# Third pair by quarters, more weight sums by adding transfers, and three more turns of zeros in a tuned encoder block

## The chip, the cores and the metric

The kernel runs on one core of one Trainium2 chip, in one launch. The time is device microseconds of that core, the median of three runs. The engines named below are PE (the matrix engine; PEld is its weight load), DVE (vector), ACT (scalar), POOL (GpSimd) and SP, whose queue issues the loads.

## The reference

The block works on 512 positions of 1024 features in float32:

```python
h = h + 0.5 * swiglu(rmsnorm(h, ffn1_norm), ffn1_w_in, ffn1_w_out)   # "first layer", D_FF = 2816
z = rmsnorm(h, mix_norm) @ w_in
h = h + concat([conv_module(z...), gated_linear_attention(z...)]) @ w_out
h = h + 0.5 * swiglu(rmsnorm(h, ffn2_norm), ffn2_w_in, ffn2_w_out)   # "second layer"
h = h + sigmoid(rmsnorm(h, ple_norm) @ w_gate) * (p @ w_proj)
out = rmsnorm(h, final_norm)

def swiglu(x, w_in, w_out):
    gate, up = split(x @ w_in, 2)
    return (silu(gate) * up) @ w_out
```

The change touches the two `swiglu` layers and the start of the kernel.

## The kernel before

**Numbers in two parts.** A float32 operand is held as a high part (rounded to the type that PE multiplies fast) and a low part, the rest. A product is three matmuls: high by high, high by low, low by high. The high part of a weight tile is a cast on ACT (`high`, tile `wh`), the low part a subtraction on DVE (`low`, tile `wl`). In place of DVE's subtraction stands in some places `added`: ACT writes the negated raw tile into `wl`, rounded by that tile's type, and POOL issues a transfer that adds the raw tile there, which leaves the rest:

```python
def added(w):
    h3, l3, r3 = w
    act.mul(l3, r3, -1.0)
    pool.dma_start(out=l3.bitcast(F32), in_=r3, accum_op=ALU.add)
    return w
```

An added low part costs ACT one more pass and DVE nothing, and the raw tile stays taken until the transfer has landed.

**Pairs.** The 2816 hidden features are 22 blocks of 128. Two blocks of gate and the two of up make a pair; there are eleven, numbered 0 to 10. A pair's product (1024 x 512 of weights by 1024 x 512 of x) is done in one of two ways:

- *Plain* (`plain_unit`, units `h0` to `h7`): eight units of 12 matmuls with 512 columns. A unit's weights are one of four raw tiles `a11`, `a12` (gate, features 0 to 511 and 512 to 1023), `a21`, `a22` (up).
- *By quarters* (Winograd's form of Strassen's product, units `m1` to `m7`, in the order m1, m2, m6, m7, m5, m4, m3, with the m1 and m2 of the next pair in between): seven products of 24 matmuls with 256 columns. It needs sums of weights (`s1` = a21 + a22 and `s2` = s1 - a11 in tiles `sm`; `s3` = a11 - a21 and `s4` = a12 - s2 in place in the raw tile) and sums of x (`t1` to `t4`, made by `Right` once for a layer: `pieces` on ACT, `sums1` and `sums2` on DVE, all in tiles `xg`, then `split` into two parts). `m1`, `m6`, `m5` and `m3` add up in one bank of PSUM, and ACT copies its state out after m1 (`sq`), m6 (`u2`, the tile `u` in the profile) and m5 (`sq`). The next product that adds into the bank waits for the copy.

Pair 0 is special in both layers and done before the others. Behind each pair its product goes through silu, the gate and a split (`act_parts`, tiles `actH`, `actL`); groups of two pairs then go through pieces of the second projection (`second`), 24 matmuls of 512 columns each, called blocks below, which are interleaved with the units. Each block adds into `h` by DVE.

**Order.** PE, ACT and DVE run in the order in which the program calls them, and so does SP. `drive` walks a list of units; every unit names jobs ("before") with a distance: a job of distance 4 is called four units ahead. Within a unit's turn the jobs go first, larger distance first, then what the last unit left over (its silu or product), then the unit's matmuls and the copy behind them, then its hook.

```python
before = [(AHEAD + (kind == 'm5'), lambda: p.part(part))] if part else []
...
before += [(9, lambda: p.fetch("a21", "a22")), (6, p.s12)]
```

AHEAD is 4. `part` is `high` and `low`, `add_part` is `high` and `added`. Raw weights have six buffers, `wh` and `wl` six each, PSUM seven banks and one more.

In the first layer (`ffn` with plain `(1, 2)`) pairs 1 and 2 are plain and quarters start at pair 3; in the second (plain `()`) quarters start at pair 1. At the start `warm_up` lets PE turn an identity tile while x loads (ten turns, then four), and the units `take` do pair 0 as x comes in.

All engine calls go through the class `Ordered`, so nearly every instruction of the profile stands under line L46, and one tells them apart by their tiles: `wh<-wr` is a cast of a raw weight tile, `wl<-wr,wh` a low part, `wl<-sm,wh` that of s1 or s2, `sm<-` the sums s1 and s2, `wr<-` s3 and s4, `hgH,wh` matmuls with x itself, `t1H` to `t3H` those with its sums, `actH,wh` blocks of the second projection, `ax<-ident` the turns of zeros.

Of the kernel before, what the change touches and what calls it, by code (L numbers as in the profile page):

```python
# [62 lines left out]
def block_kernel(ctx: ExitStack, tc: tile.TileContext, a: dict, out: bass.AP):  # L63
# [16 lines left out]
    def nm(s):  # L80
        uid[0] += 1
        return f"{s}_{uid[0]}"
# [10 lines left out]
    def tmp(s, w=SEQ, dt=F32, bufs=2):  # L93
        return tp.tile([P, w], dt, tag=s, bufs=bufs, name=nm(s))

    def bank():
        return pp.tile([P, SEQ], F32, tag="mm", bufs=7, name=nm("ps"))

    def aux():
        return pp.tile([P, SEQ], F32, tag="aux", bufs=1, name=nm("ax"))  # L100
# [15 lines left out]
    def columns(names, n, tile_name, queue):  # L116

        row = cp.tile([n, P], F32, name=tile_name + "r")
        col = cp.tile([P, n], F32, name=tile_name)
        r0 = 0  # L120
        for name, m in names:
            queue.dma_start(out=row[r0:r0 + m, :], in_=a[name][0].rearrange("(r p) -> r p", p=P))
            for c in range(m):
                vcols[name, c] = col[:, r0 + c:r0 + c + 1]
            r0 += m

        def turn():
            ps = aux()
            pe.transpose(ps[:, 0:n], row, ident[:n, :n])
            dve.tensor_copy(col, ps[:, 0:n])  # L130

        return turn
# [7 lines left out]
    def warm_up(n):  # L140
        idle = aux()
        for _ in range(n):
            pe.transpose(idle[:, 0:P], ident, ident)

    warm_up(10)
    turn_vec = columns(vecs[:1], 8, "vcol1", nc.scalar)

    def split(src, s, alloc=bt):
# [34 lines left out]
    def high(r3):  # L183

        nk, nc_ = r3.shape[1], r3.shape[2]
        hi = wp.tile([P, 1024], F32R, tag="wh", bufs=6, name=nm("wh"))
        lo = wp.tile([P, 1024], F32R, tag="wl", bufs=6, name=nm("wl"))
        h3 = hi[:, :nk * nc_].rearrange("p (k c) -> p k c", k=nk)
        l3 = lo[:, :nk * nc_].rearrange("p (k c) -> p k c", k=nk)
        act.copy(h3, r3)  # L190
        return h3, l3, r3

    def low(w, engine=dve):
        h3, l3, r3 = w
        engine.tensor_tensor(out=l3, in0=r3, in1=h3.bitcast(F32), op=ALU.subtract)
        return h3, l3
# [62 lines left out]
    def spread(col, copy=True):  # L259

        ps = aux()
        for j in range(TB):
            pe.transpose(ps[:, j * P:(j + 1) * P], col[:, j:j + 1].to_broadcast([P, P]), ident)
        if not copy:
            return ps
        bc = tmp("bc", bufs=1)
        act.copy(bc, ps)
        return bc
# [17 lines left out]
    class Norm:  # L286
        def __init__(self, engine=dve):
            self.engine = engine
            self.acc = bt(s="sqacc")
            self.n = 0  # L290
# [17 lines left out]
    def mul(ps, w, x, first, last, ks=range(4)):  # L308

        (wh, wl), k0 = w, ks[0]  # L310
        for k in ks:
            xh, xl = x[k]
            for i in range(2):
                cs = slice(i * P, (i + 1) * P)
                o = ps[:, i * HALF:(i + 1) * HALF]
                end = last and k == ks[-1] and i == 1
                pe.matmul(o, wh[:, k - k0, cs], xh, start=(first and k == ks[0] and i == 0), stop=False, skip_group_check=True)
                pe.matmul(o, wh[:, k - k0, cs], xl, start=False, stop=False, skip_group_check=True)
                pe.matmul(o, wl[:, k - k0, cs], xh, start=False, stop=end, skip_group_check=True)
# [68 lines left out]
    class Left:  # L388


        def __init__(self, w, f):
            self.w, self.f, self.done = w, f, {}

        def fetch(self, *names):
            for name in names:
# [10 lines left out]
        def part(self, name, engine=None):  # L406

            if name not in self.done:
                self.done[name] = low(high(getattr(self, name)), engine or dve)
            return self.done[name]  # L410

        def add_part(self, *names):

            for name in names:
                self.done[name] = added(high(getattr(self, name)))[:2]
# [21 lines left out]
    ffn1_in = a["ffn1_w_in"][0]  # L437
    hT = [big.tile([P, SEQ], F32, tag="H", bufs=DC, name=nm("h")) for _ in range(DC)]
    hg, xps, xt, squares = [], [], {}, []
# [12 lines left out]
    def turn_x(c):  # L452
        ps = bank()
        for t in range(TB):
            pe.transpose(ps[:, t * P:(t + 1) * P], xt[c][t], ident)
        xps.append(ps)
# [57 lines left out]
    w1 = Left(ffn1_in, 2)  # L514
# [5 lines left out]
        nc.sync.dma_start(out=made[2][i * RANK:(i + 1) * RANK, :], in_=a["gate_w_up"][0])  # L520
    turn_vec()
    turn_x(0)
    warm_up(4)
    ps0 = [bank() for _ in range(4)]
    split_w(0, 1, dve.tensor_copy)
    split_x(0)
    mid = []
# [22 lines left out]
    xb = Right(hg, "ffn1_norm")  # L550
    steps = xb.steps()
# [30 lines left out]
    AHEAD = 4  # L582
# [18 lines left out]
        for f in left:  # L601
            f()

    def ffn(w_in, w_out, x, gname, given, first, rsb, hooks, plain):


        norm = Norm()
# [3 lines left out]
        start = 1 + len(plain)  # L611
        held = []
        end = npair - 1
        pairs = {i: given.get(i) or Left(w_in, 2 * i) for i in range(npair)}
# [9 lines left out]
        def silu(g):  # L624
            s = tmp("s")
            act.activation(s, g, AF.Silu)
            return s
# [37 lines left out]
        def m2(p):  # L665
            p.y = bank()
            mul(p.y, p.part("a12"), x.op["b21"], True, True)

            def gate0():
                p.s0 = silu(plus(p.y, p.a, 0, "g1"))  # L670

            if p is pairs[start] and not plain:
                held.append(gate0)
                return []
            return [gate0]
# [51 lines left out]
        def unit(kind, i):  # L727
            p = pairs[i]

            def go(run):  # L730
                left = run(p)
                hooks.get((kind, i), lambda *_: None)()
                return left

            if kind[0] == "h":
                j = int(kind[1])
                part, run = (f"a{1 + j // 4}{1 + j % 2}", plain_unit(j)) if j % 4 < 2 else (None, plain_unit(j))
                if part:
                    return [(AHEAD, lambda: p.part(part)), (9, lambda: p.fetch(part))], lambda: go(run)
            else:  # L740
                part, run = USES[kind]
            before = [(AHEAD + (kind == 'm5'), lambda: p.part(part))] if part else []
            if kind in ("m1", "m2"):
                before.append((7, lambda: p.fetch(part)))
            elif kind == "m6":
                before += [(9, lambda: p.fetch("a21", "a22")), (6, p.s12)]
            elif kind in ("m7", "m3"):
                before.append((6, p.s3_ if kind == "m7" else p.s4_))

            return before, lambda: go(run)  # L750
# [80 lines left out]
        for i in range(start, npair):  # L831
# [3 lines left out]
            if i == end:  # L835
                half, rest = second(cut_of[i])
# [30 lines left out]
    w_in = a["w_in"][0]  # L867
    w_ahead = []

    def sums_hooks(x, names, at):  # L870

        h = {}
        for name, key in zip(names, at):
            h[key] = lambda *_, name=name: x.split(name)
        return h

    hooks = sums_hooks(xb, ("t2", "t3", "t1", "t4"), (("h5", 1), ("h7", 1), ("h3", 2), ("m1", 3)))
    hooks.update({("h%d" % (i + 1), 1): f for i, f in enumerate(steps[2:])})
    hooks.update({("m5", 3): lambda *_: made[0](), ("m5", 4): lambda *_: constants(),
                  ("m4", 10): lambda *_: w_ahead.append(ahead(w_in, D_CONV, 2 * P)),  # L880
                  ("last", 4): lambda *_: w_ahead.append(ahead(w_in, 0, 2 * P))})
    hg, norm = ffn(ffn1_in, a["ffn1_w_out"][0], xb, "mix_norm", {0: Left(ffn1_in, 0), 1: w1},
                   (ps0[:2], ps0[2:]), lambda: spread(mid[0]), hooks, (1, 2))
    pool.on = False
    cw, gwu, mean, mask, nbias = made

# [61 lines left out]
    mid = []  # L948
# [10 lines left out]
    rs, rsb = mid  # L959
# [16 lines left out]
    for k0 in range(0, DC, 4):  # L976
        for i in range(2):
            for j in range(4):
                pe.matmul(ps[2 * RANK * j:2 * RANK * (j + 1)], gw[:, k0 + j, :], hg[k0 + j][i].bitcast(F32),
                          start=(k0 == i == 0), stop=(k0 + i == 5), skip_group_check=True)  # L980
# [337 lines left out]
    ffn2_in = a["ffn2_w_in"][0]  # L1318
    wf = {i: Left(ffn2_in, 2 * i) for i in range(3)}
    w0, w1 = wf[0], wf[1]  # L1320
# [40 lines left out]
    norm = Norm()  # L1361
# [26 lines left out]
    for k in range(4):  # L1388
        for n in range(3):
            w, ps = half[n]  # L1390
# [28 lines left out]
    hg = nhg  # L1419
# [11 lines left out]
    mid = []  # L1431
    xb = Right(hg, "ffn2_norm")
    steps = xb.steps()
    steps[0]()
    w1.fetch("a21", "a22")
    w2 = wf[2]
    w2.fetch("a11", "a12")
    g0 = plain_block(w0, 0, 0)
    steps[1]()
    steps[2]()  # L1440
    u0 = plain_block(w0, 1, 0, {4: lambda: mid.append(norm.rows())})
# [4 lines left out]
    g1_ = plain_block(w0, 0, 1, {1: lambda: mid.append(spread(mid[0]))})  # L1446
# [5 lines left out]
    u1_ = plain_block(w0, 1, 1)  # L1452
# [3 lines left out]
    hooks = sums_hooks(xb, ("t4",), (("m2", 1),))  # L1456
# [3 lines left out]
    q11, q21, q12, q22, b11, b21, t2, wproj = ([] for _ in range(8))  # L1460
# [59 lines left out]
    def todo(*fs):  # L1520
# [5 lines left out]
                  ("rest", 2): todo((q_high, b21, q21, 0), (first_sum, 0), (third_sum, 0)),  # L1526
                  ("rest", 4): todo((q_high, b21, q21, 1), (first_sum, 1), (third_sum, 1)),
                  ("rest", 6): todo((final_in,), (row_sums, 0))})
    hg, norm = ffn(ffn2_in, a["ffn2_w_out"][0], xb, "ple_norm", wf, ((g0, u0), (g1_, u1_)), mid[1], hooks, ())

# [4 lines left out]
    a11, a12, a21, a22 = of_rows(0, 0), of_rows(1, 0), of_rows(0, 1), of_rows(1, 1)  # L1537
# [162 lines left out]
    t1, t3 = q11, q12  # L1700
    n2_ = [x for jp in range(2) for x in split_rows(n2, jp)]
    project(0)
    m1 = [kept(p_, "sq", bufs=3) for p_ in x_]
# [98 lines left out]
```

## Time and profile before

| | us |
|---|---|
| median of three runs | 949.27 |
| lowest and highest | 948.17, 949.77 |
| the profiled execution's own time | 948.38 |
| span of the profile (first to last instruction) | 946.7 |
| PE busy | 935.0 (99%) |
| DVE busy | 755.6 (80%) |
| ACT busy | 477.0 (50%) |
| POOL busy | 57.2 (6%) |

The profile is of one execution; its own time is 1.7 us more than its span. In rows of the time line the columns are the start, the time taken, engine, line, operation, tiles written and read, shape and count, and in brackets the idle time of the engine before it with what ended it. A row with "x4" stands for four instructions merged. Matmuls are pipelined: one takes longer than the distance to the next.

### The profile page before, as it was taken

To read this page: it belongs to the slowest core of one execution; us is meant where nothing else is said; L and a number is where in the kernel's file an instruction comes from. 1 tells how busy PE (TensorE), PEld (TensorE's weight loads), DVE (VectorE), ACT (ScalarE), POOL (GpSimd) and SP (SyncE) were. 2 spreads that over 40 slices of the span, in tenths; PEclk is the share of its full clock that TensorE was granted. 3 is DMA by queue.
4 is the path that set the end of the run, shared out by engine and by line. 5 is a ranking of instruction groups with operands and counts; after the bars stand their busy time and mean duration, and the time that the engine had idled before them with its cause. 6 is when DMAs were issued, how large, how long until landed. Compare 5 with 4: busy or idle time off the path is not lost.

```text
span 946.7 us, 14553 instructions
## 1 busy us (share of the span) xinstructions
PE 935.0 (99%) x5842; PEld 831.1 (88%) x5842; DVE 755.6 (80%) x1030; ACT 477.0 (50%) x720; POOL 57.2 (6%) x72
## 2 busy tenths in 40 slices
PE   9999999999999999999999999999999999999996
PEld 7888999999999988788877889899999999998885
DVE  5876887887788566999986788887878787866896
ACT  5652544434433574463564874444434433445882
POOL 0000200000000110001030020000000000000121
PEclk9999999999999999999999999999999999999998
DMA  7532323342323593346552572332243224347463
GB/s 229 180 114 72 106 69 117 105 131 80 103 90 111 140 257 83 81 102 167 134 126 77 154 163 82 112 114 88 90 134 112 67 91 133 96 147 225 89 113 110
DMA packets 107831, 113.43 MB, mean 120 GB/s; under 512 B 5155, under 2 KB 96469, under 8 KB 107764
## 3 DMA queue, kind: packets, MB, share of 16 engines
q1 hardware_dynamic: 101732, 94.67, 32.3%
q0 software_dynamic: 6016, 17.83, 10.4%
q8 instruction: 46, 0.75, 0.3%
q14 instruction: 21, 0.17, 0.1%
q10 hardware_dynamic: 16, 0.00, 0.0%
HBM read 93.61 MB, written 2.10 MB: 101 GB/s over the span
## 4 chain that ended last, share of the span: by engine, by line
PE 96%; DVE 2%; ACT 1%; issue 1%; POOLq 0%; POOL 0%; DVEq 0%; ACTq 0%
PE ps L46 94%; PE ax L46 2%; DVE wl L46 1%; DVE g L46 0%; ACT wh L46 0%; DVE u L46 0%; DVE wr L46 0%; ACT s L46 0%; DVE y L46 0%; DVE sm L46 0%; DVE actL L46 0%; DVE hgL L46 0%; ACT wl L46 0%; POOLq L1798 0%; ACT ycH L46 0%
## 5 line engine op out<-in xcount | busy, mean ns | idle before, releaser
L46 PE MATMUL ps<-hgH,wh 128*128 128x256 f32 (+1 forms) x768 | 235.9, 312 | 0.0
L46 PE MATMUL ps<-hgL,wh 128*128 128x256 f32 (+1 forms) x768 | 234.2, 310 | 0.0
L46 PE MATMUL ps<-hgH,wl 128*128 128x256 f32 (+1 forms) x768 | 234.0, 310 | 0.0
L46 DVE TENSOR_TENSOR wl<-wr,wh 128x1024 fp32r<-128x1024 f32 (+2 forms) x162 | 189.6, 1181 | 48.1 <-ACT wh L46 48.0
L46 ACT CAST wh<-wr 128x1024 fp32r<-128x1024 f32 (+2 forms) x177 | 177.8, 1019 | 39.8 <-PE ps L46 19.8
L46 PEld LDWEIGHTS ps<-hgH,wh 128*128 128x128 f32 x768 | 146.9, 192 | 9.9 <-issue 1.1
L46 PEld LDWEIGHTS ps<-hgH,wl 128*128 128x128 f32 x768 | 146.7, 191 | 7.8
L46 PEld LDWEIGHTS ps<-hgL,wh 128*128 128x128 f32 x768 | 146.3, 191 | 8.0 <-issue 0.2
L46 PE MATMUL ps<-actH,wh 128*128 128x512 f32 x352 | 137.4, 390 | 0.0
L46 PE MATMUL ps<-actL,wh 128*128 128x512 f32 x352 | 137.3, 390 | 0.0
L46 PE MATMUL ps<-actH,wl 128*128 128x512 f32 x352 | 136.9, 389 | 0.0
L46 ACT ACTIVATE s<-g 128x512 f32<-128x512 f32 x48 | 30.4, 633 | 190.2 <-DVE g L46 190.2
L46 DVE SCALAR_TENSOR_TENSOR cv<-glu,cw,cv 128x502 f32<-128x502 f32 (+24 forms) x120 | 81.0, 731 | 0.6
L46 PEld LDWEIGHTS ps<-actH,wl 128*128 128x128 f32 x352 | 66.1, 188 | 14.0
L46 PEld LDWEIGHTS ps<-actH,wh 128*128 128x128 f32 x352 | 66.2, 188 | 13.0
L46 PEld LDWEIGHTS ps<-actL,wh 128*128 128x128 f32 x352 | 66.2, 188 | 12.4
L46 DVE SCALAR_TENSOR_TENSOR h<-ps,h 128x512 f32<-128x512 f32 x80 | 53.9, 686 | 21.3 <-PE ps L46 21.2
L46 ACT COPY sq<-ps 128x512 f32<-128x512 f32 x40 | 23.3, 585 | 68.4 <-PE ps L46 68.3
L46 DVE TENSOR_TENSOR wl<-sm,wh 128x1024 fp32r<-128x1024 f32 x40 | 48.7, 1221 | 5.1 <-ACT wh L46 4.9
L46 ACT CAST wh<-sm 128x1024 fp32r<-128x1024 f32 x40 | 41.7, 1043 | 7.0 <-DVE sm L46 4.2
L46 ACT CAST actH<-m 128x512 fp32r<-128x512 f32 x44 | 25.4, 618 | 38.5 <-DVE m L46 38.4
L46 PE MATMUL ps<-t1H,wh 128*128 128x256 f32 x144 | 40.9, 284 | 1.0 <-ACT u L46 1.0
(267 smaller groups left out, 1744.2 us busy)
## 6 DMA issues: line engine op xcount, KB each, us to landing
wr<-in_ffn_w_in SPq DMA_DIRECT2D x84, 512.0 KB
wr<-in_ffn_w_out SPq DMA_DIRECT2D x32, 512.0 KB
wr<-in_w_in SPq DMA_DIRECT2D x20, 512.0 KB
wl<-wr POOLq DMA_DIRECT2D x16, 512.0 KB, 5.5
wr<-in_ffn_w_out SPq DMA_DIRECT2D x16, 384.0 KB
wr<-in_w_out SPq DMA_DIRECT2D x8, 512.0 KB
wq<-in_ple_w_gate SPq DMA_DIRECT2D x8, 512.0 KB
wl<-wq POOLq DMA_DIRECT2D x8, 512.0 KB, 5.3
```

The lines of the kernel that those rows point to most:

```text
L46: inst = call(*args, **kwargs)
```

## The change

1. The turns of zeros at the start are eleven and six in place of ten and four.
2. In the first layer pair 2 goes by quarters too (plain `(1,)`), so quarters start at pair 2 there; its first gate is held until m5, as it is in the second layer.
3. Low parts by adding transfer in place of DVE: in the first layer a21 of pair 1, a12 and a22 of pair 2; in the second a22 of pair 2 and a11 of pair 3. Outside the plain units such a job has distance 6 in place of 4.
4. In the first layer a22 of pair 1 and a11 of pair 2 are cast in one place (distances 3 and 4) and their low part is made in another (hooks behind h2 and h4 of pair 1).
5. The first layer's sums of x move: the pieces of steps 2 and 3 stand behind h0 (before: h1 and h2), step 4 behind h4 (h3), and the splits of t2, t3, t1, t4 behind h4, h5, h7 of pair 1 and m1 of pair 2 (before: h5 and h7 of pair 1, h3 of pair 2, m1 of pair 3). The hook's call of s12 finds it done: the job of m6 has called it just before.

```diff
-    warm_up(10)
+    warm_up(11)
...
-    warm_up(4)
+    warm_up(6)
...
+        def cast(self, name):
+            self.halves[name] = high(getattr(self, name))
+
+        def rest(self, name):
+            self.done[name] = low(self.halves[name])
...
-    def ffn(w_in, w_out, x, gname, given, first, rsb, hooks, plain):
+    def ffn(w_in, w_out, x, gname, given, first, rsb, hooks, plain, adds=(), casts=()):
...
-            if p is pairs[start] and not plain:
+            if p is pairs[start]:
                 held.append(gate0)
...
                 if part:
-                    return [(AHEAD, lambda: p.part(part)), (9, lambda: p.fetch(part))], lambda: go(run)
+                    far, make = (3, p.cast) if (kind, i) in casts else (AHEAD, p.add_part if (kind, i) in adds else p.part)
+                    return [(far, lambda: make(part)), (9, lambda: p.fetch(part))], lambda: go(run)
             else:
                 part, run = USES[kind]
-            before = [(AHEAD + (kind == 'm5'), lambda: p.part(part))] if part else []
+            if (kind, i) in casts:
+                before = [(AHEAD, lambda: p.cast(part))]
+            elif (kind, i) in adds:
+                before = [(AHEAD + 2, lambda: p.add_part(part))]
+            else:
+                before = [(AHEAD + (kind == 'm5'), lambda: p.part(part))] if part else []
...
-    hooks = sums_hooks(xb, ("t2", "t3", "t1", "t4"), (("h5", 1), ("h7", 1), ("h3", 2), ("m1", 3)))
-    hooks.update({("h%d" % (i + 1), 1): f for i, f in enumerate(steps[2:])})
+    hooks = sums_hooks(xb, ("t2", "t3", "t1", "t4"), (("h4", 1), ("h5", 1), ("h7", 1), ("m1", 2)))
+    w2 = Left(ffn1_in, 4)
+    hooks.update({("h0", 1): lambda *_: [f() for f in steps[2:4]],
+                  ("h2", 1): lambda *_: w1.rest("a22"),
+                  ("h4", 1): lambda *_: [steps[4](), w2.rest("a11"), xb.split("t2")],
+                  ("h5", 1): lambda *_: [xb.split("t3"), w2.s12()]})
...
-    hg, norm = ffn(ffn1_in, a["ffn1_w_out"][0], xb, "mix_norm", {0: Left(ffn1_in, 0), 1: w1},
-                   (ps0[:2], ps0[2:]), lambda: spread(mid[0]), hooks, (1, 2))
+    hg, norm = ffn(ffn1_in, a["ffn1_w_out"][0], xb, "mix_norm", {0: Left(ffn1_in, 0), 1: w1, 2: w2},
+                   (ps0[:2], ps0[2:]), lambda: spread(mid[0]), hooks, (1,),
+                   {("h4", 1), ("m2", 2), ("m4", 2)}, {("h5", 1), ("m1", 2)})
...
-    hg, norm = ffn(ffn2_in, a["ffn2_w_out"][0], xb, "ple_norm", wf, ((g0, u0), (g1_, u1_)), mid[1], hooks, ())
+    hg, norm = ffn(ffn2_in, a["ffn2_w_out"][0], xb, "ple_norm", wf, ((g0, u0), (g1_, u1_)), mid[1], hooks, (), {("m4", 2), ("m1", 3)})
```

More of the change, by code (lines that the diff above doesn't have):

```diff
@@ L391, in __init__ @@
         def __init__(self, w, f):
-            self.w, self.f, self.done = w, f, {}
+            self.w, self.f, self.done, self.halves = w, f, {}, {}
         def fetch(self, *names):
```

## The prediction

> **What bounds the kernel now.** I read the page first: busy time, then the chain that ended last, then the chain's pieces in order of time.
>
> ```profile
> PE 935.0 (99%) x5842; PEld 831.1 (88%) x5842; DVE 755.6 (80%) x1030; ACT 477.0 (50%) x720; POOL 57.2 (6%) x72
> PE 96%; DVE 2%; ACT 1%; issue 1%; POOLq 0%; POOL 0%; DVEq 0%; ACTq 0%
> 133.56 231.23 PE ps L46 x1515
> 593.10 248.90 PE ps L46 x1728
> ```
>
> PE is the bound, and it hardly ever stands still: the last two rows are stretches of the chain, 231 and 249 us long, of matmuls alone. So a matmul saved shortens the run by its pitch, and a wait given to PE lengthens it in full; there is nothing later that absorbs either. Two questions decide: how many us of matmuls go, and whether DVE and ACT, which make every operand, still deliver in time.
>
> A matmul's pitch is read from starts. The first two rows stand 24 matmuls of 512 columns apart, the last two 72 of 256 columns.
>
> ```profile
> 62.76 0.39 PE L46 MATMUL ps<-actH,wh 128*128 128x512 f32 x1
> 68.20 0.39 PE L46 MATMUL ps<-hgH,wh 128*128 128x512 f32 x1
> 98.12 0.28 PE L46 MATMUL ps<-hgH,wh 128*128 128x256 f32 x1
> 106.75 0.28 PE L46 MATMUL ps<-t2H,wh 128*128 128x256 f32 x1
> ```
>
> That is 5.44 / 24 = 0.2267 us and 8.63 / 72 = 0.1199 us: half the columns cost 0.53 of the time.
>
> **Term 1, the matmuls of the third pair (first layer).** Plain: 8 units of 12 matmuls, 96 x 0.2267 = 21.76 us. By quarters: 7 products of 24, 168 x 0.1199 = 20.14 us. Gain 1.62 us. [...]
>
> **Term 2, the opening.**
>
> ```profile
> 1.61 2.40 PE L46 MATMUL ax<-ident 128*128 128x128 f32 x10 [1.61 <-POOL ident masks.py:199]
> 4.06 0.18 PEld L46 LDWEIGHTS ax<-ident,vcol1r 8*128 8x128 f32 x1 [0.46 <-PE ax L46]
> 5.17 1.06 PE L46 MATMUL ax<-ident 128*128 128x128 f32 x4
> 6.20 1.36 PEld L46 LDWEIGHTS ps<-hgH,wh 128*128 128x128 f32 x4 [0.36 <-ACT hgH L46]
> 6.22 2.05 PE L46 MATMUL ps<-hgH,wh 128*128 128x512 f32 x4
> 8.07 1.15 PE L46 MATMUL ps<-hgH,wl 128*128 128x512 f32 x4
> ```
>
> A turn has a pitch of about 0.21 us (four in 1.06, the last one's tail included). The eleventh turn fits into the 0.46 us before the vector's turn at 4.06: nothing. The two others need 0.42 us where PE waits 0.36 us for ACT: about +0.1 us, at most +0.2. The matmuls run at half speed until about 8.07 either way; I take +0.1, and the other case stands with the rivals.
>
> **Term 3, the waits of pair 2 in the first layer.** Today pair 2 is plain, and DVE makes the quarter sums beside 22 us of slow matmuls. Now they come beside pair 1. Rows for the prices, each a kind of work:
>
> ```profile
> 33.99 1.05 ACT L46 CAST wh<-wr 128x1024 fp32r<-128x1024 f32 x1
> 41.54 1.05 ACT L46 CAST wh<-wr 128x1024 fp32r<-128x1024 f32 x1
> 42.49 1.70 ACT L46 ACTIVATE xg<-h,vcol 128x256 f32<-128x256 f32 x4
> 43.76 2.14 DVE L46 TENSOR_TENSOR xg<-xg,xg 128x512 f32<-128x512 f32 x3
> 45.82 0.68 DVE L46 TENSOR_TENSOR g<-ps,bc 128x512 f32<-128x512 f32 x1
> 46.44 0.39 PE L46 MATMUL ps<-hgH,wh 128*128 128x512 f32 x1
> 55.89 1.29 DVE L46 TENSOR_TENSOR t2L<-xg,t2H 128x512 fp32r<-128x512 f32 x2
> 57.10 0.68 DVE L46 TENSOR_TENSOR u<-ps,bc 128x512 f32<-128x512 f32 x1
> 63.82 2.36 DVE L46 TENSOR_TENSOR wl<-wr,wh 128x1024 fp32r<-128x1024 f32 x2 [0.26 <-ACT wh L46]
> 88.05 1.22 DVE L46 TENSOR_TENSOR sm<-wr,wr 128x1024 f32<-128x1024 f32 x1
> 89.30 1.23 DVE L46 TENSOR_TENSOR sm<-sm,wr 128x1024 f32<-128x1024 f32 x1
> 101.19 0.59 ACT L46 COPY sq<-ps 128x512 f32<-128x512 f32 x1 [1.99 <-PE ps L46]
> 563.82 1.05 ACT L46 ACTIVATE wl<-wr 128x1024 fp32r<-128x1024 f32 x1
> DMA to landing us min/median/max: 4.5/5.5/9.9
> 35.00:62.00 27.00, 27.00 (x123) 22.36 (x122) 21.80 (x30) 15.27 (x26) 0.00 (x0) 1.00 0.36 111
> ```
>
> The row before the last is the adding transfers' (of POOL, into `wl`) time from issue to landing, the last a stretch of time: busy us of PE, PEld, DVE, ACT and POOL. From start to start: 1024-wide DVE work 1.14 us, 512-wide 0.60 (0.73 where it needs the one before), ACT 1024-wide 0.95, 512-wide 0.52, a copy out of PSUM 0.49.
>
> (a) a22 of pair 1. Its cast stood at 41.54, ahead of the pieces of x. Now it is queued behind eight pieces (0.40 each, from 42.49's row), and all of ACT there is some 0.2 late, as a21's negation goes ahead of the copy of the row factors: pieces from 41.7, cast from 44.9 to 45.3, low half on DVE done at 47.2 to 47.6. h5 starts at 46.44 and needs the low half in its third matmul, at 46.9. Wait 0.3 to 0.7 us.
>
> (b) m5 of pair 2. Behind that low half DVE has, in order and without a pause: the gate of h3 0.60, three sums of x 2.06, a11 1.14, t2 1.21, s1 and s2 2.39, t3 1.21, s3 1.14, a11 of pair 3 1.14, h5's output 1.32, s2's low half 1.14, t1 1.21, the low halves of s1 and s3 2.28, h7's output 1.40: 18.2 us from 47.0 to 47.4, so to 65.2 to 65.6. ACT's act_parts of pair 1 stands waiting for that last product, and behind it: cast 0.52, a22 by transfer 0.95 + 0.95, cast of a12 of pair 3 0.95, copy of m1(3) 0.49, cast of the second projection's block 0.95, and then the copy u2 of m6(2), 0.59: 5.4 us, to 70.6 to 71.1. m5 adds into the bank that u2 copies, so it cannot start before. PE is due there at 69.0: the row at 62.76 less the three plain units of pair 2 that stand before it (3 x 2.72) is 54.6, and five products of 2.88 follow. Together with (a), PE is 1.6 to 2.1 us late; I take 1.9.
>
> (c) m5 of pair 3. a22's transfer is issued at 67.7 to 68.2 and lands 4.5 to 5.5 us later; only then is its raw buffer free for a22 of pair 3, which SP's queue holds waiting, the next projection block behind it. The load is seen here:
>
> ```profile
> 78.41 0.37 SPq L176 DMA_DIRECT2D wr<-in_ffn_w_in  x1
> 79.40:81.60 2.20, 2.20 (x12) 1.81 (x11) 0.12 (x1) 0.00 (x0) 0.00 (x0) 1.00 0.75 238
> ```
>
> 238 GB/s over 2.2 us is its 512 KB: 3.1 us from issue to landing. So s1 of pair 3 starts on DVE at 75.3 to 76.8, with all of pair 2's outputs queued behind it: eight 1024-wide (9.2), three pairs of additions (4.0), two h (1.2), m4's and m3's outputs (2.8), two waits for ACT's casts (1.1), 18.3 us; then silu, a cast, a low half, the product, two casts, a cast and u2 of m6(3), 6.1 us. u2 is out at 99.7 to 101.2. PE, 1.9 us late, is due at 70.9 + 28.2 = 99.1 (six products of 2.88 and two blocks of 5.44 between). Wait 0.6 to 2.1; I take 1.2.
>
> Term 3 is +3.1 (2.2 to 4.2). After it both engines are ahead again, as they are today from pair 4 on.
>
> **What is covered.** a21 of pair 1 by transfer: cast at 33.99 (0.95), negation 1.05, so issue at 36.1, landing 40.6 to 41.6, needed at 44.1; the 9.9 us of the slowest would cost 1.9. a12 of pair 2: its cast and negation follow a22's cast and a silu, issue at about 49, landing by 55, needed at 57.7. POOL is busy 0.00 us from 35 to 62. The loads that wait for a21's buffer (a11 of pair 3 and all behind it on SP) go at 41 and are needed from 52 on.
>
> **Term 4, the second layer.** PE stands there today, and the rows say for what.
>
> ```profile
> 582.36 1.03 ACT L46 CAST wh<-sm 128x1024 fp32r<-128x1024 f32 x1
> 583.42 1.23 DVE L46 TENSOR_TENSOR wl<-sm,wh 128x1024 fp32r<-128x1024 f32 x1 [1.70 <-ACT wh L46]
> 589.08 1.22 DVE L46 TENSOR_TENSOR wl<-wr,wh 128x1024 fp32r<-128x1024 f32 x1
> 590.22 0.68 DVE L46 TENSOR_TENSOR g<-ps,bc 128x512 f32<-128x512 f32 x1
> 591.00 0.63 ACT L46 ACTIVATE s<-g 128x512 f32<-128x512 f32 x1 [2.28 <-DVE g L46]
> 591.53 1.03 ACT L46 CAST wh<-wr 128x1024 fp32r<-128x1024 f32 x1
> 592.47 0.58 ACT L46 COPY u<-ps 128x512 f32<-128x512 f32 x1
> 591.87 0.28 PE L46 MATMUL ps<-t3H,wl 128*128 128x256 f32 x1
> 593.10 0.39 PE L46 MATMUL ps<-t1H,wh 128*128 128x256 f32 x1 [0.95 <-ACT u L46]
> ```
>
> m5 of pair 2 waits for the copy u2 (592.47), which stands on ACT behind a cast, a silu and DVE's g. The change puts a11 of pair 3 (cast and negation, 1.90 us) ahead of the cast at 582.36. DVE, idle before 583.42 for that cast, starts 1.90 later. It no longer makes a11's low half (589.08, 1.14), so its g comes 0.76 later. Then a22 of pair 2 (cast and negation, 1.90) goes ahead of the cast at 591.53, which was behind u2 before. u2 ends 0.76 + 1.90 = 2.66 us later, and PE with it. Bounds: 1.9, if DVE recovers the 0.76; 3.2, with a late load. I take +2.7.
>
> **The sum.** -1.6 + 0.1 + 3.1 + 2.7 = +4.3 us on the profiled execution's 948.38: 952.7. The median of the three runs, 949.27, is 0.9 above that execution, so I forecast 953.6.
>
> **Rivals.** *Faster: DVE's work, not ACT's order, holds the waits.* Five low halves leave DVE; if that frees u2 earlier, m5's wait in the second layer (593.10 less 591.87 and a pitch, 1.1 us) goes too and pair 2 has no waits: -1.6 - 1.1 = 946.6. For it: ACT's silu at 591.00 waits for DVE. Against: each transfer adds an ACT pass ahead of u2. It decides if ACT's 2.28 and 1.70 us of idle time take the added passes, which needs another order on ACT. Chance 0.07.
>
> *Same: DVE keeps up in the first layer.* Term 3 falls to about 0.3: 950.8. It needs DVE 1.9 us ahead of (b), and its list is taken from rows. Chance 0.10.
>
> *The turns open the clock sooner.* The four matmuls from 6.22 to 8.07 take 0.46 us each, later ones 0.23. If closing the two gaps makes the higher clock come before 6.22, those four give back 0.9 us: 952.7. [...] Turns ran from 1.61 us on and the higher clock came at about 8.07, so the rows don't show what kept it away: chance 0.10.
>
> *Slower still:* one adding transfer takes the longest time seen, 9.9 us, at (c): 4.9 us more than the 5.0 taken, 958.5. Chance 0.05. The forecast has 0.68.
>
> **How the numbers follow.** Terms 3 and 4 go from 4.1 to 7.4, the opening from -0.8 to +0.2; with -1.6 that is +1.7 to +6.0, 951.0 to 955.3 on the median, and the runs before lie 0.5 above and 1.1 below their median. I take 950.2 to 956.0, which leaves out the faster rival, the slowest and a part of the tails. A change within 0.2% (1.9 us, about what a measurement of this kernel can tell from none) means below 951.2: faster 0.07, same 0.11, slower 0.82.
>
> **What would show it.** In the profile after: 256-column matmuls from about 54.6 on instead of 98.1; PE's wait before m5 of pair 2 and of pair 3 released by ACT's copies near 70 and 100; SP's load of a22 of pair 3 behind the landing of POOL's transfer; in the second layer the wait before t1 grown from 1.1 to about 3.8 us, again by ACT's u. I am wrong if PE shows no wait near 70, or the second layer's wait shrinks.

## The result, and the profile after

| | before | after |
|---|---|---|
| median, us | 949.33 | 955.66 |
| lowest and highest | 948.17, 949.77 | 954.64, 956.12 |
| the profiled execution's own time | 948.38 | 955.51 |
| span of its profile | 946.7 | 953.8 |

The change makes the kernel slower: ratio 1.0073, 95% interval 1.0059 to 1.0087. The forecast was +4.3 us; the medians differ by 6.3, the two profiled executions by 7.1. Direction and places were right; the size was not.

The page of after, its busy time and its chain that ended last:

```profile
PE 936.0 (98%) x5917; PEld 835.5 (88%) x5917; DVE 759.8 (80%) x1035; ACT 486.2 (51%) x731; POOL 59.4 (6%) x77
PE 90%; ACT 3%; DVE 3%; issue 2%; DMA 1%; POOLq 0%; POOL 0%; ACTq 0%; SPq 0%; DVEq 0%
```

PE has 168 matmuls of 256 columns in place of 96 of 512, and three more turns, and is busy only 1.0 us longer; but its share of the chain fell from 96% to 90%. So something else releases it now. The waits of PE for `u` say what (us in total, times, longest), in after and then in before:

```profile
PE ps L46 <- ACT u L46: 6.7, 3, 3.6
```

```profile
PE ps L46 <- ACT u L46: 1.0, 1, 1.0
```

Three waits for ACT's copy `u2` stand where there was one, and a short one for DVE is new. The time line of PE in after shows each as a pair of rows, the last matmul before the wait and the first behind it. The wait for DVE's `wl`, before h5 of pair 1:

```profile
45.65 0.39 PE L46 MATMUL ps<-hgL,wh 128*128 128x512 f32 x1
46.26 0.50 PE L46 MATMUL ps<-hgH,wl 128*128 128x512 f32 x1 [0.23 <-DVE wl L46]
```

Those for `u2`, before m5 of pair 2, of pair 3 (with three more rows), and of pair 2 in the second layer:

```profile
68.38 0.28 PE L46 MATMUL ps<-t3H,wl 128*128 128x256 f32 x1
69.80 0.39 PE L46 MATMUL ps<-t1H,wh 128*128 128x256 f32 x1 [1.14 <-ACT u L46]
```

```profile
97.97 0.28 PE L46 MATMUL ps<-t3H,wl 128*128 128x256 f32 x1
100.24 0.40 PE L46 MATMUL ps<-t1H,wh 128*128 128x256 f32 x1 [1.99 <-ACT u L46]
100.46 0.39 PE L46 MATMUL ps<-t1L,wh 128*128 128x256 f32 x1
100.64 0.42 PE L46 MATMUL ps<-t1H,wl 128*128 128x256 f32 x1
100.86 0.42 PE L46 MATMUL ps<-t1H,wh 128*128 128x256 f32 x1
```

```profile
595.00 0.28 PE L46 MATMUL ps<-t3H,wl 128*128 128x256 f32 x1
598.86 0.58 PE L46 MATMUL ps<-t1H,wh 128*128 128x256 f32 x1 [3.58 <-ACT u L46]
```

The distance of two starts less a pitch (0.227 us at 512 columns, 0.120 at 256) is the wait, here from starts before rounding: 0.39 before h5 of pair 1, 1.30 before m5 of pair 2, 2.15 before m5 of pair 3, and 3.74 in the second layer, where 1.11 stood before. That is +3.83 us in the first layer and +2.63 in the second, against forecasts of 3.1 and 2.7.

The three rows from 100.46 on show what the forecast lacks altogether: behind the third wait matmuls of 256 columns start 0.18 to 0.22 us apart, not 0.12. The table by stretches of time says why (busy us of PE, PEld, DVE, ACT and POOL, then PE's granted clock, the DMA share and GB/s):

```profile
97.06:100.47 3.41, 1.42 (x12) 1.22 (x12) 3.41 (x6) 2.85 (x5) 0.00 (x0) 1.00 0.00 0
100.47:103.89 3.42, 3.42 (x18) 3.42 (x18) 3.42 (x4) 1.60 (x2) 0.00 (x0) 0.50 0.00 0
103.89:107.30 3.41, 3.41 (x28) 3.22 (x28) 2.12 (x4) 1.53 (x2) 0.00 (x0) 1.00 0.72 198
595.41:598.82 3.41, 0.00 (x0) 0.00 (x0) 0.46 (x1) 3.40 (x5) 0.86 (x1) 1.00 0.00 0
598.82:602.23 3.41, 3.37 (x16) 3.37 (x17) 2.73 (x5) 2.01 (x3) 0.00 (x0) 0.50 0.81 154
```

Behind each of the two long waits the clock is 0.50 for one stretch of 3.41 us: 16 to 18 matmuls, where the stretch from 103.89 holds 28. In before the granted clock is full from 8.17 to 940.0 us. The 1.30 us wait has no such stretch behind it.

To see where the time goes, one can set the same matmuls of two kernels against each other: count back from the last one, and start at h0 of pair 1 (32.37 us in before, 31.35 in after). From there to pair 4 and on, after needs 4.13 us more than before, and the figure stays 4.13 up to the second layer; through pair 2 of that it grows to 8.26 and ends at 8.27. Less the 1.02 us by which h0 began sooner, that is 7.25, the difference of the spans but for 0.1 at the end. These two stages, the first layer's and the second layer's, are used below for every kernel.

### The profile page after: what moved, and what is told of

Its sections match the earlier page's. It is cut to its first block, busy times and chain, and to the rows that moved or that the text cites. A ratio compares the mean times of both kernels' runs of the same rounds, so it can differ in the third digit from the quotient of the medians.

```text
span 953.8 us, 14736 instructions
## 1 busy us (share of the span) xinstructions
PE 936.0 (98%) x5917; PEld 835.5 (88%) x5917; DVE 759.8 (80%) x1035; ACT 486.2 (51%) x731; POOL 59.4 (6%) x77
## 4 chain that ended last, share of the span: by engine, by line
PE 90%; ACT 3%; DVE 3%; issue 2%; DMA 1%; POOLq 0%; POOL 0%; ACTq 0%; SPq 0%; DVEq 0%
PE ps L46 89%; PE ax L46 1%; ACT wh L46 1%; DVE wl L46 1%; DVE g L46 1%; ACT xg L46 1%; DVE u L46 1%; DMA wl<-wr 0%; DMA wr<-in_ffn_w_in 0%; ACT wl L46 0%; DVE m L46 0%; ACT s L46 0%; ACT hgH L46 0%; ACT sq L46 0%; DVE y L46 0%
## 5 line engine op out<-in xcount | busy, mean ns | idle before, releaser
L46 PE MATMUL ps<-hgH,wh 128*128 128x256 f32 (+1 forms) x768 | 231.6, 307 | 0.2 <-ACT hgH L46 0.2
L46 PE MATMUL ps<-hgH,wl 128*128 128x256 f32 (+1 forms) x768 | 230.6, 305 | 0.2 <-DVE wl L46 0.2
L46 PE MATMUL ps<-hgL,wh 128*128 128x256 f32 (+1 forms) x768 | 230.8, 306 | 0.0
L46 DVE TENSOR_TENSOR wl<-wr,wh 128x1024 fp32r<-128x1024 f32 (+2 forms) x158 | 185.0, 1181 | 47.5 <-ACT wh L46 47.4
L46 DVE TENSOR_TENSOR wl<-sm,wh 128x1024 fp32r<-128x1024 f32 x42 | 51.1, 1221 | 7.3 <-ACT wh L46 7.1
L46 PE MATMUL ps<-t1H,wh 128*128 128x256 f32 x152 | 44.8, 295 | 6.7 <-ACT u L46 6.7
L46 ACT CAST wh<-sm 128x1024 fp32r<-128x1024 f32 x42 | 43.8, 1042 | 7.2 <-DVE sm L46 4.2
```

What stands on the lines that cost most here:

```text
L46: inst = call(*args, **kwargs)
```

## The experiments

They ran in three later rounds, on chips that the record numbers 14, 0 and 7. Before ran beside them and had medians of 947.79, 947.65 and 947.90 us there, some 1.5 lower than in the first pair; so a median is compared with before of its own round. "First" and "second" are the us by which a layer's stage, measured as above from the profiles, is longer than in the one profile of before. Where a kernel leaves a stage as it was in before, the two agree to 0.02 us, so the stages can be compared across the rounds.

| kernel | median | ratio to before, 95% | first | second |
|---|---|---|---|---|
| after, once more | 955.99 | 1.0078 [1.0066, 1.0091] | +4.03 | +4.15 |
| only the turns | 947.63 | 0.9995 [0.9986, 1.0004] | 0.00 | +0.02 |
| after without the second layer's transfers | 951.1 | 1.0030 [1.0018, 1.0041] | +4.01 | +0.02 |
| only the second layer's transfers | 952.02 | 1.0041 [1.0029, 1.0054] | 0.00 | +4.17 |
| after with turns in the waits | 953.54 | 1.0055 [1.0043, 1.0068] | +2.55 | +2.67 |
| second layer, a11 alone | 948.29 | 1.0009 [1.0000, 1.0017] | 0.00 | +0.79 |
| second layer, a22 alone | 951.21 | 1.0031 [1.0019, 1.0042] | 0.01 | +3.36 |
| after with the old turns | 954.99 | 1.0072 [1.0059, 1.0086] | +2.86 | +4.00 |
| after with early transfers | 945.5 | 0.9974 [0.9964, 0.9985] | -1.00 | -1.16 |
| the same, and a22 of pair 1 early | 945.31 | 0.9975 [0.9965, 0.9985] | -1.33 | -1.12 |

**Only the turns** (before with the new turns).

```diff
-    warm_up(10)
+    warm_up(11)
...
-    warm_up(4)
+    warm_up(6)
```

> The kernel before with eleven and six turns of zeros. The forecast's step (turns cost what they overhang): 949.3 + 0.1 = 949.4 us, full clock again at about 8.2 us. Rival (turns without gaps open the clock a window earlier, as at 4.9 us in the changed kernel's profile): 949.3 - 1.1 = 948.2 us.

Measured 947.63 us, 0.2 below before, the interval on both sides of 1. The turns are not what costs, and by the interval they gain at most 1.3 us.

**After without the second layer's two transfers.**

```diff
-    ... mid[1], hooks, (), {("m4", 2), ("m1", 3)})
+    ... mid[1], hooks, ())
```

> The changed kernel without the second layer's two adding transfers. Both theories give back the 2.6 us by which PE's wait before m5 of pair 2 grew there (3.74 to 1.11 us). Waits alone: 955.7 - 2.6 = 953.1 us. Waits and clock (a wait that leaves PE idle for most of a 3.41 us window drops the clock to half for the next window, 1.7 us): 955.7 - 2.6 - 1.7 = 951.4 us, and one window of half clock in the profile in place of two.

Against the first pair's before (949.3), that was +3.8 for the waits alone and +2.1 for waits and clock. Measured: 3.3 us over before, between the two, so the median by itself decides nothing: both forecasts start from after's 6.3 us over before, and in the later round below after is 8.1 over it. The profile does decide. It has one half-clock stretch, at 101.44 behind a wait of 2.04 us, and the second layer's wait is 1.10 as in before. So the first layer's stage, +4.01, is the first layer's own doing.

**Only the second layer's two transfers** (before, with `add_part` for m4 of pair 2 and m1 of pair 3 there).

```diff
-            before = [(AHEAD + (kind == 'm5'), lambda: p.part(part))] if part else []
+            if (kind, i) in adds:
+                before = [(AHEAD + 2, lambda: p.add_part(part))]
+            else:
+                before = [(AHEAD + (kind == 'm5'), lambda: p.part(part))] if part else []
...
-    ... mid[1], hooks, ())
+    ... mid[1], hooks, (), {("m4", 2), ("m1", 3)})
```

> The kernel before with the second layer's two adding transfers alone. Waits alone: 949.3 + 2.6 = 951.9 us. Waits and clock: 949.3 + 2.6 + 1.7 = 953.6 us, with one window of half clock behind the wait near 593 us.

By the same 949.3 that was +4.3 with the clock and +2.6 without. Measured +4.2, with a wait of 3.75 us and one half-clock stretch:

```profile
589.70:593.11 3.41, 1.67 (x14) 1.47 (x13) 1.17 (x2) 2.14 (x3) 0.00 (x0) 1.00 0.11 39
593.11:596.52 3.41, 1.56 (x13) 1.56 (x14) 1.83 (x2) 2.00 (x4) 0.86 (x1) 1.00 0.43 83
596.52:599.94 3.42, 3.42 (x19) 3.42 (x18) 2.97 (x4) 2.57 (x5) 0.00 (x0) 0.50 0.48 93
```

Here the wait is shared by two stretches. The one with 1.67 us of work is followed by the full clock, the one with 1.56 by half.

**After with turns in the waits.** PE turns the identity tile while it would stand: 16 turns before m5 of pair 3, 28 in the second layer. (What is called turns of zeros ahead of the result is this, `pe.transpose` of `ident`.) The turns do not put m5 off: in the profile it starts 0.05 us behind the end of `u2` in both places, as it does in after. They only keep PE at work.

```diff
         def m5(p):
+            warm_up({(1, 3): 16, (0, 2): 28}.get((len(plain), p.f // 2), 0))
             mul(p.x, p.part("s1"), x.op["t1"], False, False)
```

> The changed kernel with 16 turns of zeros on PE ahead of m5 of pair 3 in the first layer and 28 ahead of m5 of pair 2 in the second, which fill most of the two long waits and take nothing away from what ends them. Waits alone: 955.7 us, no change. Waits and clock: neither window is idle, the clock stays up, 955.7 - 3.4 = 952.3 us, with m5 starting at the same distance behind its copy u.

953.54 us, 5.7 over before where after stands 8.1 over it: 2.3 less, from medians of two rounds, where the expectation had 3.4 for the clock and nothing for the waits alone. PE's rows and then the stretches:

```profile
99.20 1.91 PE L46 MATMUL ax<-ident 128*128 128x128 f32 x16
101.25 0.39 PE L46 MATMUL ps<-t1H,wh 128*128 128x256 f32 x1
101.47 0.28 PE L46 MATMUL ps<-t1L,wh 128*128 128x256 f32 x1
101.59 0.28 PE L46 MATMUL ps<-t1H,wl 128*128 128x256 f32 x1
```

```profile
97.36:100.78 3.42, 3.42 (x32) 3.42 (x31) 3.42 (x6) 2.16 (x4) 0.00 (x0) 1.00 0.00 0
100.78:104.19 3.41, 3.27 (x27) 3.02 (x25) 3.41 (x4) 2.32 (x3) 0.00 (x0) 1.00 0.02 5
593.31:596.72 3.41, 3.41 (x32) 3.41 (x31) 1.00 (x2) 2.31 (x3) 0.00 (x0) 1.00 0.01 4
596.72:600.13 3.41, 2.88 (x25) 2.65 (x24) 1.83 (x2) 2.00 (x4) 0.86 (x1) 1.00 0.50 96
```

From the second on, the matmuls behind the turns stand 0.12 us apart, and the clock is 1.00 throughout. The stages shrink from 4.13 and 4.13 to 2.55 and 2.67: the two half-clock stretches cost 1.58 and 1.46 us, 3.0 together (1.48 each against after once more). What is left is what the other terms make: 3.83 of waits less 1.33 of matmuls (from the last kernel below) is 2.50, and the second layer's 2.63. So the clock is a cost of its own.

**The second layer's two transfers one by one.** The edit is that of both, with `{("m1", 3)}` or `{("m4", 2)}` alone.

> The kernel before with one of the second layer's two transfers, a11 of pair 3 (cast and negation, 1.90 us, ahead of the cast of s2). The wait before m5 of pair 2 should grow from 1.1 to about 1.8 us (0.76 late, because DVE's gate product comes that much later). If a half-clock window follows a wait only above some length (1.3 us had none behind it, 2.0 had one), 1.8 lies between: theory of a threshold near 2: +0.8 us over before and full clock throughout. Rival, every wait over 1.4 us costs a window: +2.5 us, with a half-clock stretch of 3.4 us right behind the wait. Rival, the wait is not lengthened by this transfer at all (ACT's idle time takes the passes): 0.

> The kernel before with the other of the second layer's transfers, a22 of pair 2 (cast and negation ahead of the copy u2). The wait before m5 of pair 2 should grow from 1.1 by 1.9 (one cast and one negation) to 3.0 us. Theory: a wait of this length also halves the clock for one window of 3.41 us, which costs 1.7 more: +3.6 us over before, with a half-clock stretch behind the wait. Rival (the wait costs only its own length): +1.9 us and full clock. Both together, this kernel and the one with a11 alone, should not add up to the 4.2 us of the kernel with both by waits alone: 0.8 + 1.9 = 2.7 is missing the window's 1.7, which comes once.

With a11 alone the wait is 1.84 us, the clock full, the stage +0.79: the theory's 0.8. With a22 alone the wait is 2.99 us as worked out, but the runs fell into two groups, 949.3 to 949.6 and 950.8 to 952.7, which neither theory had foreseen. The groups alone do not tell the two theories apart: before itself (42 runs at 947.3 to 948.6, eight at 949.2 to 949.8) and a11 alone (948.0 to 948.7 and 950.0 to 950.1) fall into two groups as well. Two more profiles of the same kernel followed.

> A second look at the kernel before with the transfer of a22 in the second layer, whose times fell into two groups (949.3 to 949.6 and 950.8 to 952.7). Theory: the same wait of 3.0 us costs a half-clock window when over half of one window of 3.41 us is idle, and none when the wait is shared out over two windows. So a profile near 949.5 shows the full clock behind the wait and less than 1.8 us of it in any window; one above 951 shows a half-clock window.

> A third look at the same kernel, with the same expectation: a half-clock window if, and only if, more than about half of one window is idle.

The stretches around the wait in the first, second and third profile of this kernel, whose wait was 2.99, 3.00 and 2.99 us:

```profile
590.65:594.06 3.41, 2.61 (x22) 2.41 (x21) 1.36 (x2) 1.96 (x3) 0.00 (x0) 1.00 0.00 0
594.06:597.48 3.42, 1.39 (x11) 1.39 (x12) 1.82 (x2) 2.01 (x4) 0.86 (x1) 1.00 0.30 57
597.48:600.89 3.41, 3.41 (x18) 3.41 (x17) 2.79 (x4) 2.41 (x4) 0.00 (x0) 0.50 0.54 101
```

```profile
590.92:594.33 3.41, 2.36 (x20) 2.16 (x18) 1.12 (x2) 2.20 (x3) 0.00 (x0) 1.00 0.00 0
594.33:597.75 3.42, 1.63 (x13) 1.63 (x14) 1.83 (x2) 2.01 (x4) 0.86 (x1) 1.00 0.37 72
597.75:601.16 3.41, 3.41 (x31) 3.41 (x30) 3.02 (x4) 2.81 (x5) 0.00 (x0) 1.00 0.47 87
```

```profile
590.57:593.98 3.41, 0.93 (x8) 0.72 (x7) 0.15 (x1) 3.41 (x5) 0.52 (x1) 1.00 0.00 0
593.98:597.40 3.42, 3.07 (x14) 3.07 (x15) 2.73 (x4) 2.01 (x4) 0.34 (x1) 0.50 0.80 153
```

The stretches are cut at multiples of 3.413 us from the moment at which the clock came on (10.38, 10.65 and 6.89 us in these three); in the first and the third the half clock begins on such a cut, at 597.48 and 593.98 us, 172 times 3.413 behind it. Where one holds only 1.39 or 0.93 us of work, half clock follows and the stage is 3.36 or 3.25 us longer. Where the emptier one holds 1.63, the clock stays and the stage is 1.85 longer, the wait's own growth of 1.88. The same wait thus cost 1.4 to 1.5 us more or less, by how it was shared out over the stretches. The bound that the expectation gave (under 1.8 us idle) held, if narrowly (3.41 less 1.63 is 1.78); the second profile's execution took 951.3 us all the same and not about 949.5; the author puts that down to its clock, which came on late, at 10.65 us.

**After once more, and after with the old turns** (11 and 6 back to 10 and 4).

> The kernel after once more, beside the same runs of before as the partial kernels. If the first layer's part and the second layer's part act alone, it stands at the sum of their ratios: +3.3 and +4.2, 7.5 us over before, with two half-clock windows in the profile. On the first chip it stood 6.3 over before; that difference again would mean that one of the two windows is not always lost.

> The kernel after with ten and four turns of zeros as before. Theory (the turns change nothing but when the clock's windows begin): within 0.5 us of the kernel after, and both kernels show openings of the clock spread over 5 to 10 us. Rival (the turns open the clock a window sooner, worth some 1 to 2 us): 1 to 2 us slower than the kernel after.

After is 8.1 us over before in this round, near the sum of its parts (3.3 + 4.2). Its profile has both half-clock stretches again, behind waits of 2.07 and 3.74 us. With the old turns after is not slower; its median is 1.0 lower, the intervals overlapping. In its profile the wait before m5 of pair 3 is the longest of all, 2.36 us, and has no half clock behind it:

```profile
96.41:99.83 3.42, 2.72 (x23) 2.52 (x21) 2.97 (x5) 1.53 (x4) 0.00 (x0) 1.00 0.00 0
99.83:103.24 3.41, 1.90 (x16) 1.90 (x17) 3.41 (x5) 3.36 (x5) 0.00 (x0) 1.00 0.00 0
103.24:106.65 3.41, 3.41 (x29) 3.23 (x28) 3.38 (x5) 1.53 (x2) 0.00 (x0) 1.00 0.24 70
```

It is shared by two stretches, with 2.72 and 1.90 us of work, and the first layer's stage is +2.86 in place of +4.13. That this is also what tells the lower medians apart (after itself has single runs of 954.6 and 954.7 among those near 956) is likely, but none of those runs was profiled.

**Early transfers.** After, with the transfers for m4 issued eight units ahead and that for m1 seven, in place of six (m2's stays at six), so that cast and negation no longer stand just ahead of `u2` on ACT. Where an m1 or m2 takes such a transfer, its raw weights are also fetched one unit sooner.

```diff
-                before = [(AHEAD + 2, lambda: p.add_part(part))]
+                before = [({"m4": 8, "m1": 7}.get(kind, 6), lambda: p.add_part(part))]
...
-                before.append((7, lambda: p.fetch(part)))
+                before.append((7 + ((kind, i) in adds), lambda: p.fetch(part)))
```

> The kernel after, with only the distances of the adding transfers outside the plain units changed: a11 (m1) at 7 and a22 (m4) at 8 units ahead in place of 6, so that cast and negation stand on ACT well ahead of the copy u2. Theory (the waits and the clock windows are all that makes the change slow): the waits before m5 of pairs 2 and 3 of the first layer and of pair 2 of the second fall from 1.3, 2.1 and 3.7 us to under 0.3 each, no half-clock window is left, and the matmuls saved and the 1.1 us of the second layer's old wait remain: 2.0 to 3.3 us faster than before. Rival (the transfers collide with other loads or POOL's work and stay slow wherever they are issued): waits of 1 us or more stay, and the time is at or above that of before.

945.5 us, ratio 0.9974 [0.9964, 0.9985]: faster than before by about 2.2 us and than after by some 10. ACT's rows in the second layer:

```profile
582.30 2.00 ACT L46 CAST wh<-wr 128x1024 fp32r<-128x1024 f32 x2
584.20 1.05 ACT L46 ACTIVATE wl<-wr 128x1024 fp32r<-128x1024 f32 x1
586.15 0.63 ACT L46 ACTIVATE s<-g 128x512 f32<-128x512 f32 x1 [0.90 <-DVE g L46]
588.86 0.63 ACT L46 ACTIVATE s<-g 128x512 f32<-128x512 f32 x1 [2.08 <-DVE g L46]
589.40 1.03 ACT L46 CAST wh<-wr 128x1024 fp32r<-128x1024 f32 x1
590.34 0.57 ACT L46 COPY u<-ps 128x512 f32<-128x512 f32 x1
```

The cast and negation of a22 now stand at 583 to 585, where ACT was waiting for DVE anyway (2.81 us at 592.16 in after, the same silu). Behind the silu at 588.86 comes one cast and then `u2`. All waits for `u2` are gone, before's own too; no half-clock stretch is left.

In the first layer the raw buffer comes free sooner as well. DVE's first sum of pair 3, s1, in after and then here:

```profile
75.80 1.23 DVE L46 TENSOR_TENSOR sm<-wr,wr 128x1024 f32<-128x1024 f32 x1 [4.44 <-DMA wr<-in_ffn_w_in]
```

```profile
71.25 1.22 DVE L46 TENSOR_TENSOR sm<-wr,wr 128x1024 f32<-128x1024 f32 x1
```

The wait of 4.44 us for the load is gone. Counted from the start of h0 (31.35 in after, 32.41 here), s1 starts 5.6 us sooner and `u2` of pair 3 ends 5.6 us sooner, more than the 1.9 of a cast and a negation. So the wait before m5 of pair 3 goes with the earlier landing, not only with the order on ACT.

**Early transfers, and a22 of pair 1 cast sooner.**

```diff
-                    far, make = (3, p.cast) if (kind, i) in casts else ...
+                    far, make = (4, p.cast) if (kind, i) in casts else ...
...
-    hooks.update({("h0", 1): lambda *_: [f() for f in steps[2:4]],
+    hooks.update({("h0", 1): steps[2], ("h1", 1): steps[3],
```

> As the kernel with early transfers, and besides the cast of a22 of pair 1 at distance 4 in place of 3 and the pieces of x one step behind h0 and the next behind h1 in place of both behind h0. This should take away the wait of 0.39 us before h5 of pair 1 as well: 0.4 us faster than the kernel with early transfers alone, 2.4 to 3.7 us faster than before. Rival: DVE, not the order on ACT, sets the low half of a22 of pair 1, and the wait stays: same time as the kernel with early transfers.

The wait before h5 is gone and the first layer's stage is 0.33 us shorter, so the order on ACT had held it; the median, 945.31, is only 0.2 lower, which this measurement can't tell from none. Its profiled run had the clock on at 10.53 us and took 947.25, so the stages say more here than that run's time. This is the fastest kernel of the study by its median.

## Why the prediction was right or wrong

**The step that failed** is in its first paragraph: "a wait given to PE lengthens it in full". It does, and two waits here did more: behind the 3.413 us stretches that they left with 1.42 and 0.00 us of PE's work, the clock was 0.50 for the next stretch. The two half-clock stretches cost 3.0 us by the kernel that fills the waits with turns, and no term of the sum had them. In the trace of before no wait does this, its one wait for `u2` being 1.11 us, but the sign is there, at the very end, where no matmul follows: the stretch from 936.60 to 940.01 us holds 1.43 us of PE's work, and the clock is 0.50 behind it. The prediction spoke of the lower clock only at the opening. In the first layer, waits of 2.04, 2.07 and 2.15 us had half clock behind them.

**Luck.** The measured 955.66 lies inside the range of 950.2 to 956.0, but above the 955.3 that the terms' upper bounds give: the room left for the scatter of runs took it in, not the mechanism. The profiled pair also had 1.0 us of the loss hidden by an early opening of the clock in after. In the later round after stands 8.1 us over before, near the 8.2 of its two stages; on the 949.3 of the first pair that would be 957.4, outside the range.

**Term 1**, -1.62: measured -1.33, in the last kernel, where no wait of the first layer is left. The 168 matmuls of 256 columns cost 20.13 us as worked out; the 512-column ones gave back 21.46, not 21.76. In before 312 of them in this stage stood 227.1 ns apart, in the last kernel the 216 left stand 228.7 apart.

**Term 2**, +0.1: the new turns alone make no difference that can be measured. In after's profile the clock came on at 4.90 us rather than 8.17, which gave 1.0 us back, but one pair can't put that down to the turns: in fourteen profiles the clock came between 4.90 and 10.65, in seven with the new turns between 4.90 and 10.53 (6.9 in the mean), in seven with the old between 6.02 and 10.65 (8.6). The rival "the turns open the clock sooner" is right for the profiled pair and not borne out by the medians.

**Term 3**, +3.1 (2.2 to 4.2): measured +3.83 in waits. (a) 0.39, inside 0.3 to 0.7, released by DVE's low half. (b) 1.30; with (a) PE is 1.69 us late, inside 1.6 to 2.1, and the releaser is the copy `u2` at 69.16. (c) was taken at 1.2 (0.6 to 2.1) and is 2.15. The two copies, and the start of the chain that leads to the second:

```profile
69.16 0.58 ACT L46 COPY u<-ps 128x512 f32<-128x512 f32 x1
99.61 0.58 ACT L46 COPY u<-ps 128x512 f32<-128x512 f32 x1
```

```profile
67.19 4.52 DMA wl<-wr
71.77 3.94 DMA wr<-in_ffn_w_in
```

The mechanism is as forecast: SP's load of a22 stands behind POOL's landing, and s1 behind the load. From the start of s1 (75.80) to the end of `u2` (99.61 and 0.58) it is 24.4 us, the 18.3 + 6.1 that were added up. To compare with the forecast's times, which are on the scale of before, add the 1.02 us by which h0 began sooner in after: PE is due at 98.09 + 1.02 = 99.1, as forecast, and `u2` ends at 101.2, the upper end of 99.7 to 101.2. The load is what was mis-sized: it took 3.94 us, not 3.1, and that 0.8 is most of the 0.95 by which the wait is longer than the 1.2 taken.

**Term 4**, +2.7: measured +2.63 in waits, and its two parts singly 0.73 (a11; forecast 0.76) and 1.88 (a22; forecast 1.90). ACT's rows show the order:

```profile
594.87 0.63 ACT L46 ACTIVATE s<-g 128x512 f32<-128x512 f32 x1 [2.08 <-DVE g L46]
595.41 1.03 ACT L46 CAST wh<-wr 128x1024 fp32r<-128x1024 f32 x1
596.34 1.05 ACT L46 ACTIVATE wl<-wr 128x1024 fp32r<-128x1024 f32 x1
597.30 1.03 ACT L46 CAST wh<-wr 128x1024 fp32r<-128x1024 f32 x1
598.23 0.57 ACT L46 COPY u<-ps 128x512 f32<-128x512 f32 x1
```

**The sum by what was measured**, from the profiled pair: -1.0 opening, -1.3 matmuls, +3.8 and +2.6 waits, +3.0 clock, together +7.1, the difference of the two executions.

**The rivals.** "Faster" fell as argued: each transfer added its passes ahead of `u2`. Its condition, another order on ACT, is what the early transfers supply, and there before's own wait goes too, as that rival had it: 1.1 us in the second layer. "Same" fell with (b). No transfer into `wl` took 9.9 us in after: 4.5 to 7.4, 5.2 in the median.

Left open: what decides when the clock first comes on, and why before is 1.5 us lower in the later rounds. The latter may be the opening too, though no run shows it: three of before's four runs beside after lie at 949.3 to 949.8, where eight of its 50 later ones do, and two later kernels whose profiled run had the clock on late (10.45 us in a11 alone, 10.53 in the last kernel) took 1.8 and 1.9 us more in it than their medians. From h0 on, the later profile of the turns alone is within 0.03 us of before's.

## What to carry to other kernels

A low part by transfer takes work from DVE, but it puts two passes on ACT (cast and negation, 1.90 us here) and holds the raw buffer until it has landed (4.5 to 7.4 us behind the issue in after): put it where ACT would wait anyway, not ahead of a copy that frees PE's bank, and early enough that the next load does not stand behind it. When costing a wait of PE, look in the trace for half clock behind it too: the half-clock stretches of 3.41 us cost 1.4 to 1.6 us each here, on top of the wait. Where the wait can't be removed, turns of the identity in it can keep the clock, as 16 and 28 of them did here. To size a part of a change, set the same matmuls of two traces against each other, since single times carry the scatter of the opening (4.90 to 10.65 us here).

## What the runs showed of the hardware

In after the granted clock is full from 4.90 us for 95.57 us, 0.50 for 3.41, full for 494.93, 0.50 for 3.41 and full for 348.16: 28, 1, 145, 1 and 102 times 3.413 us. In before it is full from 8.17 us for 931.84, 273 times 3.413. In fourteen profiles it came on at fourteen different moments, from 4.90 to 10.65 us.

Of the stretches of 3.413 us counted from there, half clock came behind those with 0.00 and 1.42 us of PE work as the profile counts it (after), 0.12 (after with the old turns), 0.93 and 1.39 (a22 alone), 1.43 (the end of before) and 1.56 (the second layer's two transfers). Full clock came behind 1.63 (a22 alone), 1.67 (the second layer's two transfers), 1.71 (the end of after) and 1.90 (after with the old turns). The same wait of 3.0 us thus cost 1.85 or about 3.3 us, and with a wait of 2.36 us, shared by two stretches, the first layer's stage was +2.86, where one of 2.15 made it +4.13. With 16 and 28 turns of the identity in the waits the clock stayed 1.00.

The opening shows no such order. A stretch with 3.31 us of PE work ahead of the clock's coming did not bring it (3.71 to 7.12 us in the last kernel), while it came behind one with 3.13 (4.25 to 7.67 in after with the old turns).

Of the types, a matmul of 512 columns with float32 operands took 0.43 us in before (two in 0.86 from 487.86), one with the rounded parts 0.227.
